# One base inverse of 128 partitions in place of two of 64, in a gated delta rule with retention

## The chip, the cores and the metric

The kernel runs on one core of a Trainium2 chip. The metric is the device time of one execution in microseconds (us); lower is better. The engines are TensorE (PE in the profile, with PEld for its weight loads), VectorE (DVE), ScalarE (ACT), GpSimd (POOL, which also issues DMAs) and SyncE (SP, which issues most loads).

## What is computed

One layer over 512 tokens of width 1024: an input projection, two mixers (a gated delta rule with 8 heads, and a retention with 4), their gated sum, and a squared-ReLU MLP. The change lies in the delta rule. Of the reference, cut to it:

```python
lower = jnp.where(strict, jnp.einsum('bhncd,bhnmd->bhncm', k_beta, k) * decay, 0.0)
t_inv = lax.linalg.triangular_solve(lower, eye, left_side=True, lower=True, unit_diagonal=True)
u = jnp.einsum('bhncm,bhnme->bhnce', t_inv, v * beta[..., None])
...
def step(state, inp):
    qe, ww, uu, aqk, kd, ld = inp
    v_new = uu - jnp.einsum('bhck,bhkv->bhcv', ww, state)
    o = jnp.einsum('bhck,bhkv->bhcv', qe, state) + jnp.einsum('bhcm,bhmv->bhcv', aqk, v_new)
    state = state * ld[..., None, None] + jnp.einsum('bhck,bhcv->bhkv', kd, v_new)
    return state, o
```

`t_inv` is the inverse of a unit lower triangular matrix for each head and each chunk of tokens. The kernel works with chunks of 128 tokens: 8 heads x 4 chunks = 32 triangular matrices of 128 x 128.

## The kernel before

All products of activations with weights are made of three matmuls (`mm3`, lines 84 to 86), from a high and a low half of each operand. `weights` loads a tile of weights on the SP queue; line 117 (ACT) and line 118 (DVE) split it into `whi` and `wlo`, which have three buffers each. `feature_major` (lines 252 to 270) takes 512 columns of weights into four PSUM banks of the pool `psm`, or 256 columns into two; the pool has four banks. A group of 512 columns is 96 matmuls of 512 columns, one of 256 columns 48.

The delta rule is the block from line 681. Its steps, in the order in which the program is written (lines 932 to 954), are:

- `keys(g4)` for four heads at a time (g4 = 0, 1): projection (for g4 = 0 it was made earlier, in `first_keys`), convolution and SiLU (`conv_silu`: a memset on POOL at line 632, two ACT copies out of the bank at 635 and 640, three taps on DVE at 642, ACT at 643, DVE at 646), transposes to token rows, squares and `rsqrt` (from line 695), decays (ACT 665, PE 666, ACT 668), the products of keys (PE 710), and on DVE `mt` (713, kept in the tile `acc`) and `kd` (716).
- `base_inverse(g4, pool)` for the 16 matrices of four heads: the four diagonal blocks of 32 x 32 of each matrix are copied through DRAM scratch so that every block has a partition of its own (64 partitions: four DMAs at line 726, one at 732), 31 elimination steps of two DVE operations each follow (741 and 747), a copy that transposes (748), and the results go back through DRAM (749 and 750, then 753 into `rt`). All these DMAs are issued by POOL.
- `double_blocks(pool, scr, m0)` for 8 matrices (two heads): it loads `rn` (765) and puts blocks of 32 together to 64 and to 128 with small matmuls (780, 786, 789, 797, 801) and DVE copies between them.
- `values_queries(g2, pool)` for a pair of heads: 512 columns of values and 256 of queries, with `conv_silu`, transposes (323), and `at` (832).
- `recurrence(g2, ...)` over the four chunks of a pair: PE 862, 871, 880, 894 and 901, with DVE and ACT operations between them.
- `gated(g2, ...)`: 512 columns of the gate in `token_major` (four banks), ACT 604 into the tile `zz`, DVE 605 and 607; then transposes and the output product `ya_partial`.

Buffers that the steps share: the `mrb` of the first inverse has the slot `zz`, that of the second lies in `acc`; the inverse's `tmp` has the slot `vn`, of one buffer, which the recurrence uses for `vn`; `rn` and `qf` share two buffers; `c_raw` and `c_y` have two each.

The order of the instructions on each engine is fixed before the run, by a planner: it goes by the order of the program (raised at places with `high_priority`), takes first what is ready and has its buffers by its own account of time, and so lets later steps run ahead of earlier ones that wait. Each engine then works through its list in order.

Of the kernel before, what the change touches and what calls it, by code (L numbers as in the profile page):

```python
# [10 lines left out]
F32 = mybir.dt.float32  # L11
# [8 lines left out]
P = 128  # L20
# [40 lines left out]
def hybrid_block_kernel(ctx: ExitStack, tc: tile.TileContext, a: dict, out: bass.AP):  # L61
    nc = tc.nc
# [299 lines left out]
    rt = pa.tile([P, 32, P], F32, name="rt")  # L362
# [318 lines left out]
    with delta_rule:  # L681
        mt = acc.rearrange("p k t -> p (k t)").rearrange("p (n c) -> p n c", c=P)
        def keys(g4, pool):
            br2 = pool.tile([P, 16], F32, tag="br2", name="br2")
            ssk = pool.tile([P, 16], F32, tag="ssk", name="ssk")
            ns = slice(16 * g4, 16 * g4 + 16)
            pss = feature_major(w_in, xs, OFF_KA + g4 * 512, 512, 8) if g4 else first_keys
            for i in range(4):
                h = 4 * g4 + i
                conv_silu(pss[i], 8 + h, kf[:, h, :], pool)  # L690
                pt = to_tokens(kf[:, h, :])
                junk = pool.tile([P, 256], BF16, tag="junk", name="junk")
                sum_squares(pt, ssk[:, 4 * i : 4 * i + 4], junk)
                nc.scalar.copy(kd[:, 4 * h : 4 * h + 4, :], pt)
            nc.vector.tensor_scalar(ssk, ssk, EPS, None, ALU.add)
            r = rsqrt(ssk, 16, "k")
            nc.vector.tensor_copy(rk[:, ns], r)
            beta_g = beta[:, :, 4 * g4 : 4 * g4 + 4].transpose([0, 2, 1])
            nc.vector.tensor_tensor(
                br[:, ns].rearrange("p (h c) -> p h c", h=4), beta_g, r.rearrange("p (h c) -> p h c", h=4), ALU.mult  # L700
            )
            nc.vector.tensor_tensor(br2, br[:, ns], r, ALU.mult)
            nc.vector.tensor_tensor(rinv[:, ns], r, ssk, ALU.mult)
            for i in range(4):
                h = 4 * g4 + i
                dt = decays(h, pool)
                pk = psx.tile([P, 4, P], F32, tag="dl", name="dl", bufs=3)
                for c in range(4):
                    kc = kf[:, h, c * P : (c + 1) * P]
                    nc.tensor.matmul(pk[:, c, :], kc, kc, start=True, stop=True)  # L710
                for c in range(4):
                    n = 4 * h + c
                    nc.vector.scalar_tensor_tensor(
                        mt[:, n, :], pk[:, c, :], br2[:, 4 * i + c : 4 * i + c + 1], dt[:, c, :], ALU.mult, ALU.mult
                    )
                    nc.vector.tensor_scalar(
                        kd[:, n, :], kd[:, n, :], rk[:, n : n + 1], dt[:, c, P - 1 : P], ALU.mult, ALU.mult
                    )

        def base_inverse(g4, pool):  # L720

            scr_m, scr_r, scr_t = (dr.tile([4, 16, 1024], F32, tag=f"scr{i}", name="scr") for i in range(3))
            ns = slice(16 * g4, 16 * g4 + 16)
            for b in range(4):
                bs = slice(32 * b, 32 * b + 32)
                nc.gpsimd.dma_start(scr_m[b].rearrange("n (m c) -> m n c", m=32), mt[bs, ns, bs])
            if g4 == 0:
                mrb = pool.tile([64, 2, 1024], F32, tag="zz", name="mrb")
            else:
                mrb = acc[0:64, 0:4, :].rearrange("p (i k) t -> p i (k t)", i=2)  # L730
            mb, rb = mrb[:, 0, :], mrb[:, 1, :]
            nc.gpsimd.dma_start(mb, scr_m.rearrange("b n e -> (b n) e"))
            nc.gpsimd.memset(rb, 0.0)
            nc.gpsimd.memset(rb[:, 0:1024:33], 1.0)
            tmp = pool.tile([64, 256], F32, tag="vn", name="tmp")
            mb3 = mb.rearrange("p (m c) -> p m c", m=32)
            rb3 = rb.rearrange("p (c i) -> p c i", c=32)
            for j in range(31):
                nr, ni = 31 - j, j + 1
                t3 = tmp[:, : nr * ni].rearrange("p (c i) -> p c i", c=nr)  # L740
                nc.vector.tensor_tensor(
                    t3,
                    mb3[:, j, j + 1 : 32].unsqueeze(2).to_broadcast([64, nr, ni]),
                    rb3[:, j, 0:ni].unsqueeze(1).to_broadcast([64, nr, ni]),
                    ALU.mult,
                )
                nc.vector.tensor_tensor(rb3[:, j + 1 : 32, 0:ni], rb3[:, j + 1 : 32, 0:ni], t3, ALU.subtract)
            nc.vector.tensor_copy(mb3, rb3.transpose([0, 2, 1]))
            nc.gpsimd.dma_start(scr_r.rearrange("b n e -> (b n) e"), rb)
            nc.gpsimd.dma_start(scr_t.rearrange("b n e -> (b n) e"), mb)  # L750
            for b in range(4):
                bs = slice(32 * b, 32 * b + 32)
                nc.gpsimd.dma_start(rt[bs, ns, bs], scr_t[b].rearrange("n (m c) -> m n c", m=32))
            return scr_r

        pool_marks = []
# [1 line left out]
        def double_blocks(pool, scr_r, m0):  # L758

            rn = pool.tile([P, 8, 64], F32, tag="qf", name="rn", bufs=2)  # L760
            nc.gpsimd.memset(rn, 0.0)
            for b in range(3):
                bs = slice(32 * b, 32 * b + 32)
                cs = slice(32 * (b % 2), 32 * (b % 2) + 32)
                mark = nc.gpsimd.dma_start(
                    rn[bs, :, cs], scr_r[b, m0 % 16 : m0 % 16 + 8].rearrange("n (m c) -> m n c", m=32)
                )
            pool_marks.append(mark)

            def bank(w):  # L770
                ps = psx.tile([P, T], F32, tag="dl", name="dl", bufs=3)
                return ps[:, : 8 * w].rearrange("p (n c) -> p n c", n=8)

            pairs = [(slice(b, b + 32), slice(b + 32, b + 64)) for b in (0, 64)]
            ns = slice(m0, m0 + 8)
            y = pool.tile([P, 8, 64], F32, tag="dt", name="y")
            p1 = bank(32)
            for lo, hi in pairs:
                for n in range(8):
                    nc.tensor.matmul(p1[hi, n, :], mt[lo, m0 + n, hi], rn[lo, n, 0:32], start=True, stop=True)  # L780
            for lo, hi in pairs:
                nc.vector.tensor_copy(y[hi, :, 0:32], p1[hi])
            p2 = bank(32)
            for lo, hi in pairs:
                for n in range(8):
                    nc.tensor.matmul(p2[lo, n, :], y[hi, n, 0:32], rt[hi, m0 + n, hi], start=True, stop=True)
            hi = slice(32, 64)
            for n in range(8):
                nc.tensor.matmul(p2[hi, n, :], rt[hi, m0 + n, hi], y[hi, n, 0:32], start=True, stop=True)
            for lo, hi in pairs:  # L790
                nc.vector.tensor_scalar(rt[lo, ns, hi], p2[lo], -1.0, None, ALU.mult)
            hi = slice(32, 64)
            nc.vector.tensor_scalar(rn[hi, :, 0:32], p2[hi], -1.0, None, ALU.mult)
            lo, hi = slice(0, 64), slice(64, 128)
            p3 = bank(64)
            for n in range(8):
                nc.tensor.matmul(p3[hi, n, :], mt[lo, m0 + n, hi], rn[lo, n, :], start=True, stop=True)
            nc.vector.tensor_copy(y[hi], p3[hi])
            p4 = bank(64)
            for n in range(8):  # L800
                nc.tensor.matmul(p4[lo, n, :], y[hi, n, :], rt[hi, m0 + n, hi], start=True, stop=True)
            nc.vector.tensor_scalar(rt[lo, ns, hi], p4[lo], -1.0, None, ALU.mult)
# [127 lines left out]
            gate_rows(pss, rows, lambda t: zz[:, t, :])  # L930

        keys(0, pa2)
        scr = base_inverse(0, pa2)
        vq = values_queries(0, pa2)
        keys(1, pa2)
        double_blocks(pa2, scr, 0)
        og = None
        for g2 in range(4):
            rows = recurrence(g2, vq, pa2)
            if g2 == 0:  # L940
                double_blocks(pa2, scr, 8)
                scr = base_inverse(1, pa2)
            if g2 < 3:
                vq = values_queries(g2 + 1, pa2)
            if g2 == 1:
                double_blocks(pa2, scr, 16)
                double_blocks(pa2, scr, 24)
            if g2 in (1, 2):
                add_blocks(pool_marks[-1], 8 + 2 * g2)
            gated(g2, rows, pa2)  # L950
            if g2:
                ya_partial(g2 - 1, og)
            og = gated_features(rows, lambda f: na[:, f % 2 : f % 2 + 1])
# [467 lines left out]
```

## Time and profile before

| | us |
|---|---|
| time, three runs | 1362.62, 1362.79, 1366.61 (median 1362.79) |
| profiled execution, first to last instruction | 1362.5 |
| PE busy | 1347.0 |
| DVE busy | 912.8 |
| ACT busy | 651.7 |
| POOL busy | 109.4 |
| matmul instructions | 6685 |

The profiled execution's own time is its span, 1362.5 us; its execution is not told apart from the three in the first row, and what lies outside the span is about 0.3 us against the median. Busy time is the union of an engine's instructions. A row of a timeline has the start, the duration, the engine, the line, and "output<-inputs"; a row of groups has the count, the busy time and the mean of one in ns, and the idle time ahead of it with what ended it. In a row of waits stand the total, the number and the longest.

### The profile page before, as it was taken

How to read it: one execution, taken by the hardware profiler on the slowest of the kernel's cores; microseconds unless marked ns; L12 is line 12 of the kernel's file. 1: busy time of each engine (PE TensorE's matmuls, PEld its weight loads, DVE VectorE, ACT ScalarE, POOL GpSimd, SP SyncE). 2: the span in 40 equal slices, each digit the busy share in tenths (PEclk: the TensorE clock that was granted, in tenths of full speed). 3: DMA queues.
4: the chain of work that ended last, by engine and by line, in shares of the span. 5: the costliest groups of instructions: out<-in, count | busy, mean ns of one | idle time of the engine just before them, and what ended most of it. 6: DMA issues, size and time to landing. Idle time of an engine off the chain costs nothing.

```text
span 1362.5 us, 17876 instructions
## 1 busy us (share of the span) xinstructions
PE 1347.0 (99%) x6685; PEld 1110.7 (82%) x6685; DVE 912.8 (67%) x1606; ACT 651.7 (48%) x1204; POOL 109.4 (8%) x161
## 2 busy tenths in 40 slices
PE   9999999999999999999999999999999999999997
PEld 7888787788877888888888888888889888888886
DVE  5799899864665557567477577575775744828535
ACT  5977564624543322453453343343355736436441
POOL 2010310121011002000000100011101100000000
PEclk9999999999999999999999999999999999999999
DMA  5254715379458447775584782488639843625421
GB/s 178 64 154 133 202 43 180 117 153 238 108 124 169 110 147 158 190 240 193 131 255 132 192 263 93 154 217 182 199 117 238 224 154 110 197 95 169 132 86 62
DMA packets 101718, 214.70 MB, mean 158 GB/s; under 512 B 7158, under 2 KB 20624, under 8 KB 101120
## 3 DMA queue, kind: packets, MB, share of 16 engines
q1 hardware_dynamic: 85616, 170.41, 39.1%
q0 software_dynamic: 15280, 42.03, 17.0%
q8 instruction: 52, 0.85, 0.3%
q10 hardware_dynamic: 736, 1.12, 0.2%
q14 instruction: 34, 0.28, 0.1%
HBM read 207.77 MB, written 64.49 MB: 200 GB/s over the span
## 4 chain that ended last, share of the span: by engine, by line
PE 89%; DVE 5%; DMA 2%; ACT 2%; issue 1%; DVEq 0%; ACTq 0%
PE mm L84 18%; PE mm L85 18%; PE mm L86 18%; PE mm L242 10%; PE dl L242 10%; PE tr L323 3%; PE mm L456 2%; DVE wlo L118 1%; PE dl L86 1%; PE dl L85 1%; PE dl L84 1%; PE dl L901 1%; PE dl L871 1%; DVE c_y L642 1%; PE dl L880 1%; PE dl L862 1%
## 5 line engine op out<-in xcount | busy, mean ns | idle before, releaser
L118 DVE TENSOR_TENSOR wlo<-raw,whi 128x1024 fp32r<-128x1024 f32 x245 | 298.8, 1221 | 269.0 <-ACT whi L117 267.7
L117 ACT CAST whi<-raw 128x1024 fp32r<-128x1024 f32 x245 | 257.4, 1052 | 428.9 <-PE mm L85 243.4
L84 PE MATMUL mm<-actT,whi 128*128 128x512 f32 x480 | 190.1, 396 | 0.0
L85 PE MATMUL mm<-actT,whi 128*128 128x512 f32 x480 | 189.9, 396 | 0.0
L86 PE MATMUL mm<-actT,wlo 128*128 128x512 f32 x480 | 189.0, 395 | 0.0
L84 PEld LDWEIGHTS mm<-actT,whi 128*128 128x128 f32 x480 | 90.2, 188 | 18.7 <-ACT c_y L640 0.8
L86 PE MATMUL mm<-hn,wlo 128*128 128x512 f32 (+1 forms) x288 | 105.4, 366 | 0.0
L85 PE MATMUL mm<-hn,whi 128*128 128x512 f32 (+1 forms) x288 | 105.3, 366 | 0.0
L84 PE MATMUL mm<-hn,whi 128*128 128x512 f32 (+1 forms) x288 | 105.3, 366 | 0.0
L86 PEld LDWEIGHTS mm<-actT,wlo 128*128 128x128 f32 x480 | 90.3, 188 | 17.9
L85 PEld LDWEIGHTS mm<-actT,whi 128*128 128x128 f32 x480 | 90.3, 188 | 17.8
L84 PE MATMUL mm<-og,whi 128*128 128x512 f32 x256 | 99.7, 390 | 1.0 <-DVE zz L605 1.0
L85 PE MATMUL mm<-og,whi 128*128 128x512 f32 x256 | 99.6, 389 | 0.0
L86 PE MATMUL mm<-og,wlo 128*128 128x512 f32 x256 | 99.6, 389 | 0.0
L242 PE MATMUL mm<-whi,xsum 128*128 128x512 f32 x256 | 80.8, 389 | 0.0
L642 DVE SCALAR_TENSOR_TENSOR c_y<-c_raw,convw,c_y 128x512 f32<-128x512 f32 x96 | 69.7, 743 | 2.4 <-ACT c_y L640 1.8
L85 PEld LDWEIGHTS mm<-hn,whi 128*128 128x128 f32 x288 | 54.3, 189 | 8.8
L84 PEld LDWEIGHTS mm<-hn,whi 128*128 128x128 f32 x288 | 54.3, 189 | 8.7
L86 PEld LDWEIGHTS mm<-hn,wlo 128*128 128x128 f32 x288 | 54.3, 189 | 8.7
L84 PE MATMUL mm<-whi,actT 128*128 128x512 f32 x152 | 61.1, 402 | 0.1
L242 PE MATMUL dl<-whi,actT 128*128 128x512 f32 x192 | 61.1, 389 | 0.0
L242 PE MATMUL dl<-whi,ffq 128*128 128x512 f32 x192 | 61.0, 389 | 0.0
(345 smaller groups left out, 2608.8 us busy)
## 6 DMA issues: line engine op xcount, KB each, us to landing
raw<-in_w_in_dram SPq DMA_DIRECT2D x101, 512.0 KB, 4.3
raw<-sums SPq DMA_DIRECT2D x56, 512.0 KB, 4.2
raw<-in_w_up_dram SPq DMA_DIRECT2D x36, 512.0 KB, 4.6
sums<-in_w_in_dram SPq DMA_DIRECT2D x32, 512.0 KB, 5.6
sums<-sums POOLq DMA_DIRECT2D x28, 512.0 KB, 7.1
raw<-in_w_down_dram SPq DMA_DIRECT2D x26, 512.0 KB, 3.8
sums<-in_w_down_dram SPq DMA_DIRECT2D x24, 512.0 KB, 7.4
raw<-in_w_br_a_dram SPq DMA_DIRECT2D x16, 512.0 KB, 4.0
```

What stands on the lines that cost most here:

```text
L84: nc.tensor.matmul(ps, lh, rh, start=first, stop=False)
L85: nc.tensor.matmul(ps, lh, rl, start=False, stop=False)
L86: nc.tensor.matmul(ps, ll, rh, start=False, stop=last)
L117: nc.scalar.copy(hi[:, :n], raw[:, :n])
L118: nc.vector.tensor_tensor(lo[:, :n], raw[:, :n], hi[:, :n], ALU.subtract)
L242: m = nc.tensor.matmul(pss[t], lhs[i // 2], rhs[i % 2], start=first and k + i == 0, stop=k + i == 5, skip_group_check=not first,)
L323: nc.tensor.transpose(ps, src, ident)
L456: nc.tensor.matmul(ps[:, ts], ws[w][:, kk, f * P : (f + 1) * P], xs[x][:, k, ts], start=first and kk + i == 0, stop=kk == len(ks) - 1 and ...
L642: nc.vector.scalar_tensor_tensor(y, raw[:, j : j + T], tap(j), y, ALU.mult, ALU.add)
L862: nc.tensor.matmul(ks[:, hh, :], kf[:, h0 + hh, cs], state[:, hh, :], start=True, stop=True)
L871: nc.tensor.matmul(px[:, hh, :], rt[:, nn[hh], :], vx[:, hh, :], start=True, stop=True)
L880: nc.tensor.matmul(pc[:, hh, :], kd[:, nn[hh], :], vn[:, hh, :], start=True, stop=True)
```

## The change

The two inverses of 64 partitions become one of 128 partitions, for all 32 matrices. It stands behind `keys(0)` and `keys(1)`, which are now next to one another; `values_queries(0)` comes after it. The call behind the first recurrence goes. The stores into the scratch and the loads into `rt` stay as small as they were, and are eight each in one call. `mrb` has the slot `zz`.

```diff
-        def base_inverse(g4, pool):
-
-            scr_m, scr_r, scr_t = (dr.tile([4, 16, 1024], F32, tag=f"scr{i}", name="scr") for i in range(3))
-            ns = slice(16 * g4, 16 * g4 + 16)
+        def base_inverse(pool):
+
+            scr_m, scr_r, scr_t = (dr.tile([4, 32, 1024], F32, tag=f"scr{i}", name="scr", bufs=1) for i in range(3))
             for b in range(4):
                 bs = slice(32 * b, 32 * b + 32)
-                nc.gpsimd.dma_start(scr_m[b].rearrange("n (m c) -> m n c", m=32), mt[bs, ns, bs])
-            if g4 == 0:
-                mrb = pool.tile([64, 2, 1024], F32, tag="zz", name="mrb")
-            else:
-                mrb = acc[0:64, 0:4, :].rearrange("p (i k) t -> p i (k t)", i=2)
+                for g4 in range(2):
+                    ns = slice(16 * g4, 16 * g4 + 16)
+                    nc.gpsimd.dma_start(scr_m[b, ns].rearrange("n (m c) -> m n c", m=32), mt[bs, ns, bs])
+            mrb = pool.tile([P, 2, 1024], F32, tag="zz", name="mrb")
...
-            tmp = pool.tile([64, 256], F32, tag="vn", name="tmp")
+            tmp = pool.tile([P, 256], F32, tag="vn", name="tmp")
...
-                    mb3[:, j, j + 1 : 32].unsqueeze(2).to_broadcast([64, nr, ni]),
-                    rb3[:, j, 0:ni].unsqueeze(1).to_broadcast([64, nr, ni]),
+                    mb3[:, j, j + 1 : 32].unsqueeze(2).to_broadcast([P, nr, ni]),
+                    rb3[:, j, 0:ni].unsqueeze(1).to_broadcast([P, nr, ni]),
...
-            for b in range(4):
-                bs = slice(32 * b, 32 * b + 32)
-                nc.gpsimd.dma_start(rt[bs, ns, bs], scr_t[b].rearrange("n (m c) -> m n c", m=32))
+            for g4 in range(2):
+                ns = slice(16 * g4, 16 * g4 + 16)
+                for b in range(4):
+                    bs = slice(32 * b, 32 * b + 32)
+                    nc.gpsimd.dma_start(rt[bs, ns, bs], scr_t[b, ns].rearrange("n (m c) -> m n c", m=32))
...
-                    rn[bs, :, cs], scr_r[b, m0 % 16 : m0 % 16 + 8].rearrange("n (m c) -> m n c", m=32)
+                    rn[bs, :, cs], scr_r[b, m0 : m0 + 8].rearrange("n (m c) -> m n c", m=32)
...
         keys(0, pa2)
-        scr = base_inverse(0, pa2)
+        keys(1, pa2)
+        scr = base_inverse(pa2)
         vq = values_queries(0, pa2)
-        keys(1, pa2)
         double_blocks(pa2, scr, 0)
         og = None
         for g2 in range(4):
             rows = recurrence(g2, vq, pa2)
             if g2 == 0:
                 double_blocks(pa2, scr, 8)
-                scr = base_inverse(1, pa2)
```

## The prediction

> **What bounds the kernel now.** The page comes first, for the engine that is never free.
>
> ```profile
> span 1362.5 us, 17876 instructions
> ...
> PE 1347.0 (99%) x6685; PEld 1110.7 (82%) x6685; DVE 912.8 (67%) x1606; ACT 651.7 (48%) x1204; POOL 109.4 (8%) x161
> ```
>
> TensorE (PE) is busy for 99% of the span, VectorE (DVE) for 67%. The change leaves the matmuls as they are, so it can win only what PE now idles, and can lose by making PE idle. The windows by stage show where the idling is (columns: window, its length, then busy us of PE, PEld, DVE, ACT, POOL, granted clock, DMA share, GB/s). The stage of the delta rule, to which every changed line belongs, is 60 to 440 us; the first base inverse lies in 89 to 139, the second in 186 to 237.
>
> ```profile
> 89.00:139.00 50.00, 49.38 (x245) 39.95 (x245) 49.06 (x137) 37.51 (x112) 5.02 (x11) 1.00 0.44 139
> ...
> 186.00:237.00 51.00, 50.38 (x303) 40.53 (x303) 48.19 (x137) 26.78 (x63) 4.36 (x6) 1.00 0.46 146
> ...
> 60.00:440.00 380.00, 375.84 (x2120) 303.24 (x2119) 292.65 (x668) 207.16 (x498) 55.10 (x90) 1.00 0.57 146
> ```
>
> PE idles 380.00 - 375.84 = 4.2 us in the whole stage, 0.6 us around the second inverse. DVE is full in both windows (49.06 of 50, 48.19 of 51), yet PE hardly notices: it runs matmuls of later steps ahead of time. The list of PE's waits agrees; these are its longest in this stage, and the only one that touches the second inverse:
>
> ```profile
> PE dl L880 <- ACT vn L875: 1.2, 1, 1.2
> ...
> PE tr L323 <- DVE vt L607: 0.6, 1, 0.6
> ```
>
> So the question is not how much DVE work goes, but whether PE still has enough work to run ahead on while it waits for the one inverse that is left.
>
> **The change part by part.** *Removed: the second inverse.* Its 31 pairs and its copy, and, for the price of 128 instead of 64 partitions, one copy of each kind out of PSUM:
>
> ```profile
> L741 DVE TENSOR_TENSOR tmp<-acc 64x31 f32<-64x31 f32 (+15 forms) x31 | 10.2, 330 | 0.3
> L747 DVE TENSOR_TENSOR acc<-acc,tmp 64x31 f32<-64x31 f32 (+15 forms) x31 | 10.2, 329 | 0.2
> ...
> L748 DVE COPY acc<-acc 64x1024 f32<-64x1024 f32 x1 | 1.1, 1066 | 0.0
> ...
> L798 DVE COPY y<-dl 64x512 f32<-64x512 f32 x4 | 2.8, 695 | 4.0 <-PE dl L797 4.0
> L890 DVE COPY st<-dl 128x512 f32<-128x512 f32 x4 | 2.7, 686 | 3.2 <-PE dl L880 3.2
> ```
>
> 695 ns on 64 partitions, 686 on 128: the one inverse on 128 costs what one on 64 did, and 10.2 + 10.2 + 1.1 = 21.5 us of DVE goes. What it is worth to the end is what PE waited there: at most the 0.6 us above. I take -0.6. On the GpSimd queue (POOL) one load and two stores go (4 + 1 + 2 + 4 DMAs twice become 8 + 1 + 2 + 8) and two memsets; POOL is 8% busy: nothing.
>
> *Moved: keys(1) ahead of the inverse.* Now the inverse starts as soon as keys(0) is done; its chain, as POOL, DVE and the chain of work show it:
>
> ```profile
> 76.24 2.61 POOL L726 DMA_DIRECT2D scr<-acc  x4 [24.05 <-DVE kd L716]
> ...
> 83.91 0.56 POOL L732 DMA_DIRECT2D mrb<-scr  x1 [0.69 <-DMA scr<-acc]
> ...
> 138.00 1.03 POOL L749 DMA_DIRECT2D scr<-mrb  x1 [7.88 <-DVE br L702]
> ...
> 141.99 1.21 POOL L765 DMA_DIRECT2D rn<-scr  x2 [2.24 <-DMA scr<-mrb]
> ```
>
> ```profile
> 88.78 0.17 DVE L741 TENSOR_TENSOR tmp<-mrb 64x31 f32<-64x31 f32 x1
> ...
> 137.79 1.13 DVE L748 COPY mrb<-mrb 64x1024 f32<-64x1024 f32 x1
> ```
>
> ```profile
> 148.22 0.23 PE mm L86
> 148.45 0.24 PE mm L84
> 148.69 0.62 PE dl L780 x16
> ```
>
> From the last kd to the first step: 88.78 - 76.24 = 12.5 us. The steps: 138.9 - 88.8 = 50.1 us, of which 21.5 are its own (the first inverse has the same instructions); DVE puts other work between every two. From its end to the first matmul of double_blocks(0) on PE (line 780): 148.7 - 138.9 = 9.8 us.
>
> When will keys(1) be done? It takes the place that the values of head pair 0 have now: four convolutions whose last DVE step is the first row below. Then come the squares (the second and third row, keys(1) now: 132.7 - 130.0 = 2.7 us) and the chain of rsqrt, mt and kd (keys(0) now: from the fourth row to 76.2, 15.6 us).
>
> ```profile
> 92.76 0.68 DVE L646 SCALAR_TENSOR_TENSOR c_y<-c_raw,c_y 128x512 f32<-128x512 f32 x1
> ...
> 129.29 0.67 DVE L646 SCALAR_TENSOR_TENSOR kf<-c_raw,c_y 128x512 f32<-128x512 f32 x1
> ...
> 132.69 0.18 DVE L695 TENSOR_SCALAR ssk<-ssk 128x16 f32<-128x16 f32 x1 [0.28 <-ACT junk L657]
> ...
> 60.58 0.17 DVE L695 TENSOR_SCALAR ssk<-ssk 128x16 f32<-128x16 f32 x1
> ```
>
> 93.4, less some 2 us of inverse steps and vt products between these convolutions today, is 91.5; + 2.7 + 15.6 = 110. The inverse begins at 110 + 12.5 = 122.5, or a little later, since each bulk transfer now has 512 KB. Nearest rows (KB, median us to landing):
>
> ```profile
> mrb<-scr POOLq DMA_DIRECT2D x1, 256.0 KB, 4.3
> acc<-scr POOLq DMA_DIRECT2D x1, 256.0 KB, 5.8
> ...
> sums<-sums POOLq DMA_DIRECT2D x28, 512.0 KB, 7.1
> ```
>
> Between +0 and +2.8 us each way (7.1 - 4.3; the last adds while it lands); I take +1, nearer to the rows of the same tile. The Trainium skill (DMA: Bandwidth & Descriptors, section Anatomy of one DMA) gives 2.0 us plus bytes / 436e3 for such a transfer, an estimate of 2.6 us for 256 KB, where the row has 4.3, and 0.6 us more for 512 KB: by it the sum would be 0.8 us lower in all. The eight small stores are issued 0.65 us apart (2.61 / 4); the four of heads 0 to 3 can go early. Start: 123.5.
>
> How long the steps take has two ends: alone 21.5 us, or 50.1 as now. In between lie the values and queries of pair 0, whose convolutions wait until then, and the wlo splits that feed PE; DVE was full in the same way, so I take the row, 50. End 173.5; + 9.8 + 1 gives double_blocks(0) at about 184 instead of 148.7.
>
> *What covers PE until then.* Matmuls between the start of the first of these groups and double_blocks(0), and those of the gate of pair 0, by line 84 (85 and 86 issue as many):
>
> ```profile
> L84 PE MATMUL mm<-actT,whi 128*128 128x512 f32 x119 | 47.3, 398 | 0.0
> ```
>
> ```profile
> L84 PE MATMUL mm<-whi,actT 128*128 128x512 f32 x32 | 13.5, 421 | 0.0
> ```
>
> Before the recurrence there are 144 + 96 + 144 = 384 matmuls (pair 0, keys(1), pair 1). 119 x 3 less two not begun, 355, are done at 148.65; 29 and the gate's 96 are left, 125 x 0.23 (each one's time in the chain above) = 28.8 us, and four groups of transposes of pair 1's values, 4 x 0.44 = 1.8 us by such a group in the chain:
>
> ```profile
> 156.77 0.44 PE tr L323 x4
> ```
>
> 148.7 + 28.8 + 1.8: PE is covered until 179. It then waits 184 - 179 = 5 us; behind line 780 in its queue stand the rest of double_blocks(0) and the recurrence of pair 0, and everything of later pairs waits for these. After that the gate's banks empty into zz, which the inverse has just released (mrb has its slot), and the values of pair 2 fill the gaps of double_blocks and the recurrence: 0.
>
> *The banks.* keys(1) and the values of pair 0, with four PSUM banks each, now follow one another; today the queries, with two, stand between.
>
> ```profile
> L84 PE MATMUL mm<-actT,whi 128*128 128x512 f32 x45 | 17.8, 397 | 0.0
> ```
>
> ```profile
> 83.58 0.69 ACT L640 ACTIVATE c_y<-mm,convw 128x512 f32<-128x512 f32 x1
> ```
>
> 133 matmuls (45 + 44 + 44) have run by 82.4. Afterwards PE could run 96 of keys(1) and, in the two free banks and with three weight buffers, 36: the same point. The third bank comes free at 83.58 + 0.69 = 84.3. That is 1.9 us, less two groups of transposes of 0.44: +1.
>
> Sum: 1362.5 - 0.6 + 5 + 1 = 1367.9, and the runs' median (1362.79) lies 0.3 above the profiled span: **1368**.
>
> **Rivals.** *The cover holds.* The inverse stands ahead of the other DVE work in the program's order, and with keys(1) done there is less to put between. If its steps take under 45 us, the blocks come by 179 and only the banks' 1 us is left: 1362 to 1366. For it speaks the end of the first inverse, where sixteen steps took the 6.5 us from 131.2 to 137.75 (their groups in that window stand below); against it, that DVE had no gap in 89 to 139.
>
> ```profile
> L741 DVE TENSOR_TENSOR tmp<-mrb 64x192 f32<-64x192 f32 (+7 forms) x8 | 2.2, 274 | 0.0
> L747 DVE TENSOR_TENSOR mrb<-mrb,tmp 64x192 f32<-64x192 f32 (+7 forms) x8 | 2.2, 273 | 0.0
> ```
>
> *The banks do not empty.* The gate needs four banks, and those of pair 1 leave only as its convolutions run, on a DVE that the inverse holds until 173. POOL can do the same: its line 749 waits for the inverse's end, and a c_raw memset (line 632) that is planned behind it holds up the convolution that needs it. Today's sign of a bank that waits for DVE:
>
> ```profile
> 155.46 0.58 ACT L635 COPY c_raw<-mm 128x512 f32<-128x512 f32 x1 [2.47 <-DVE c_y L646]
> ```
>
> If two banks are blocked, only 36 of the gate's 96 matmuls can run ahead, and 60 x 0.23 = 13.8 us of cover falls away: 1368 + 13.8 = 1381.8, 1376 to 1382 with part of it. It decides as soon as fewer than about 80 of the 96 run before double_blocks(0).
>
> *Faster.* Today the recurrence of pair 1 starts and then stands still, since its vn shares the buffer of the inverse's tmp:
>
> ```profile
> 209.24 1.03 PE L871 MATMUL dl<-vt,rt 128*128 128x256 f32 x4
> ```
>
> ```profile
> 236.39 0.84 ACT L875 ACTIVATE vn<-dl,br 128x256 f32<-128x256 f32 x2
> ```
>
> Without the second inverse these 27 us go, pair 1 to 3 come earlier, and the waits at the stage's end can close. The bound is all of the stage's idle time, 4.2 us: 1358.3 if no new wait comes. It decides if the blocks of pair 0 come by 179 and the later waits of over 1 us vanish.
>
> *A slower clock.* PE's granted clock is 1.00 in every window above; before it is warm, the first matmuls of the same 512 columns take longer:
>
> ```profile
> L381 PE MATMUL warm<-warm 128*128 128x512 bf16 x18 | 8.0, 630 | 1.3 <-DVE warm L370 1.3
> ```
>
> A wait that cools PE would cost 630 - 398 = 232 ns on each matmul until it is warm (398 from the row of line 84 above); if that lasts for eight, 1.9 us: 1370. The longest wait here, 1.3 us, shows nothing of it. The Trainium skill (TensorE: Matmul & The Clock Gate, section Why this matters for your kernels) says that an idle gap over some 3 us drops the clock to half; no run here shows it yet, and my 5 us in one piece would be the first.
>
> That the change does not do what it says, because 128 partitions cost twice as much, the two copies above exclude.
>
> **How the numbers follow.** 0.3% (4.1 us) is about what a measurement of this kernel can tell from no change. Chances: the forecast, a wait of 3 to 9 us, 0.37; with the slower clock 0.05; the cover holds 0.29; the banks 0.20; faster 0.09. Slower by over 0.3% (above 1366.9): 0.05 + 0.20 + 0.33 of the forecast = 0.58. Faster (below 1358.7): 0.07 of the last. Within: 0.35. The range must take in the cover's 1362 and reach into both ends: 1360 to 1380 leaves out about 0.08 at the bottom and 0.10 at the top.
>
> **What would show it.** The page: DVE 21 us less busy, PE's busy time the same, the span longer. Steps 741 and 747 once, on 128 partitions, at 330 ns each, starting near 123 and ending near 173. Line 780 first near 184, with a PE wait of about 5 us ahead of it. An idle second at 82 to 85. The recurrence of pair 1 without a gap between lines 871 and 875. It is wrong if line 780 comes before 175, if PE's waits in 60 to 190 sum to under 2 us, or if the gate's matmuls stand still for full banks.

## The result, and the profile after

The changed kernel takes 1377.07 us (median of 4 runs, 1375.37 to 1380.57), the kernel before 1362.70 us beside it (4 runs, 1361.72 to 1366.61): a ratio of 1.0102, 95% interval 1.0083 to 1.0122. The change makes the kernel 1% slower. The forecast had the sign and the place of the loss; its size, 5.3 us, is too small against 14.4. The profiled execution is the slowest of the four, 1380.57 us with a span of 1378.9; the others' spans are 1373.6 to 1375.4, 3.5 to 5.3 us less. What follows accounts for the 16.4 us between the two profiled spans (1378.9 - 1362.5), 2 us more than lie between the medians. How long the wait at line 780 is in the three shorter executions, no trace shows.

The first two parts of the page of the changed kernel:

```profile
span 1378.9 us, 17806 instructions
...
PE 1351.6 (98%) x6685; PEld 1114.2 (81%) x6685; DVE 894.8 (65%) x1543; ACT 651.0 (47%) x1204; POOL 103.1 (7%) x156
...
PEclk9999989999999999999999999999999999999999
```

VectorE has 18.0 us less to do (912.8 - 894.8; 21 were forecast), and the span is longer. The row of the clock has an 8 in the slice from 172 to 207 us. The windows, with the columns of the prediction, put the loss in the stage of the delta rule, in two places:

```profile
89.00:139.00 50.00, 46.90 (x233) 37.95 (x232) 44.59 (x111) 35.73 (x99) 5.43 (x13) 1.00 0.55 162
60.00:440.00 380.00, 365.88 (x2048) 295.41 (x2047) 264.81 (x586) 197.55 (x475) 46.03 (x82) 0.98 0.53 138
```

```profile
181.00:184.00 3.00, 0.20 (x1) 0.00 (x0) 1.22 (x1) 1.04 (x1) 0.00 (x0) 0.86 1.02 397
184.00:187.00 3.00, 0.00 (x0) 0.00 (x0) 1.10 (x2) 1.73 (x4) 2.71 (x5) 0.50 1.04 338
187.00:190.00 3.00, 0.00 (x0) 0.00 (x0) 1.38 (x3) 0.33 (x1) 2.34 (x4) 0.50 1.08 361
190.00:194.00 4.00, 3.89 (x23) 3.28 (x24) 0.00 (x0) 0.00 (x0) 1.86 (x3) 0.50 0.56 109
194.00:198.00 4.00, 4.00 (x13) 3.12 (x13) 0.00 (x0) 0.00 (x0) 0.00 (x0) 0.65 0.00 0
198.00:202.00 4.00, 4.00 (x19) 3.34 (x18) 1.22 (x1) 1.05 (x1) 0.00 (x0) 1.00 0.00 0
```

TensorE now idles 14.1 us of the stage (380.00 - 365.88) instead of 4.2. Of that, 8.8 lie in 181 to 190, where it does next to nothing and the DMA share is above 1. After that it is busy, but at a clock of 0.50 and 0.65: in 194 to 198 it starts 13 matmuls, in 198 to 202, at 1.00, 19. TensorE's longest waits in the stage say for what:

```profile
PE dl L780 <- DMA rn<-scr: 8.9, 1, 8.9
PE mm L86 <- DVE wlo L118: 1.8, 1, 1.8
PE tr L323 <- DVE mrb L745: 0.9, 1, 0.9
...
PE dl L871 <- ACT junk L908: 0.7, 1, 0.7
```

The first is the forecast's wait at line 780, 8.9 us for 5. The path of the inverse on GpSimd's queue, on VectorE and on TensorE (the steps are lines 739 and 745 now, the copy 746, the stores 747 and 748, the loads of rn 765):

```profile
112.66 2.57 POOL L727 DMA_DIRECT2D scr<-acc  x4 [2.05 <-DVE kd L716]
118.99 0.10 POOL L632 MEMSET c_raw<- 128x3 f32 x1 [3.76 <-DVE c_y L646]
...
120.36 0.57 POOL L730 DMA_DIRECT2D mrb<-scr  x1 [0.67 <-issue]
...
177.22 1.01 POOL L747 DMA_DIRECT2D scr<-mrb  x1 [9.88 <-DVE mrb L745]
...
184.29 1.21 POOL L765 DMA_DIRECT2D rn<-scr  x2 [5.36 <-DMA scr<-mrb]
```

```profile
126.45 0.19 DVE L739 TENSOR_TENSOR tmp<-mrb 128x31 f32<-128x31 f32 x1 [1.73 <-DMA mrb<-scr]
...
176.95 1.15 DVE L746 COPY mrb<-mrb 128x1024 f32<-128x1024 f32 x1
```

```profile
180.81 0.39 PE L86 MATMUL mm<-whi,actT 128*128 128x512 f32 x1
190.11 1.03 PE L780 MATMUL dl<-rn,acc 32*32 32x32 f32 x16 [8.91 <-DMA rn<-scr]
...
192.51 0.63 PE L84 MATMUL mm<-actT,whi 128*128 128x512 f32 x1
192.94 0.63 PE L85 MATMUL mm<-actT,whi 128*128 128x512 f32 x1
...
197.28 0.39 PE L84 MATMUL mm<-actT,whi 128*128 128x512 f32 x1
```

The last stores of mt go out at 112.7, the steps begin at 126.45 and their copy ends at 178.10, and line 780 begins at 190.11. Cover ended at 181.2. Then matmuls start 0.43 us apart until 197, and 0.23 apart from there.

The account of the 16.4 us goes by the two pages. TensorE is idle for 27.3 us of the span (1378.9 - 1351.6) instead of 15.5 (1362.5 - 1347.0), 11.8 more, and the same 6685 matmuls keep it busy for 4.6 us more (1351.6 - 1347.0). Of the idle time 8.9 us are the wait at line 780; the other 2.9 are the small waits of this kernel less those of the kernel before. Of the 4.6, some 3 are the slow clock from 190.11 to 197.05 (13 matmuls of 0.43 in place of 0.23 are 2.6, the first ones are a little worse). Some 1.5 us more come from a second slow stretch, in which seven matmuls start 0.43 us apart or more. No wait of over 0.7 us stands between the two:

```profile
240.00:245.00 5.00, 5.00 (x60) 3.85 (x57) 3.10 (x10) 2.15 (x10) 0.00 (x0) 0.66 0.00 0
```

### The profile page after: what moved, and what is told of

It reads as the page before. It is cut to its first block, busy times and chain, and to the rows that moved or that the text cites. A ratio compares the mean times of both kernels' runs of the same rounds, so it can differ in the third digit from the quotient of the medians.

```text
span 1378.9 us, 17806 instructions
## 1 busy us (share of the span) xinstructions
PE 1351.6 (98%) x6685; PEld 1114.2 (81%) x6685; DVE 894.8 (65%) x1543; ACT 651.0 (47%) x1204; POOL 103.1 (7%) x156
## 4 chain that ended last, share of the span: by engine, by line
PE 84%; DVE 7%; DMA 4%; ACT 3%; issue 2%; DVEq 0%; ACTq 0%; POOL 0%; POOLq 0%; SPq 0%
PE mm L84 17%; PE mm L85 17%; PE mm L86 17%; PE mm L242 10%; PE dl L242 9%; PE tr L323 2%; PE mm L456 2%; DVE wlo L118 2%; DVE c_y L642 1%; PE dl L871 1%; PE dl L84 1%; PE dl L86 1%; PE dl L85 1%; PE dl L901 1%; PE dl L880 1%
## 5 line engine op out<-in xcount | busy, mean ns | idle before, releaser
L84 PE MATMUL mm<-actT,whi 128*128 128x512 f32 x480 | 192.9, 402 | 0.1
L85 PE MATMUL mm<-actT,whi 128*128 128x512 f32 x480 | 191.5, 399 | 0.0
```

Of the source, the lines that this page charges most:

```text
L84: nc.tensor.matmul(ps, lh, rh, start=first, stop=False)
L85: nc.tensor.matmul(ps, lh, rl, start=False, stop=False)
```

## The experiments

The theory after the result: the steps on VectorE, in their new place, end too late for the cover; the round trip of the blocks through DRAM is stretched by full DMA engines; the wait lowers the clock. The rivals: the new order of the keys itself costs the time, or the transfers of 512 KB do, or the work is only badly divided between VectorE and GpSimd.

**The steps left out.** The changed kernel with no step at all: its 32x32 blocks stay identities, so this kernel leaves the base of the inverse out. Order, tiles and transfers stay.

```diff
-            for j in range(31):
+            for j in range(0):
```

> The changed kernel without the 31 elimination steps (the computation is cut: the inverse of the 32 x 32 blocks is left as the identity); the order, the one inverse's transfers and its copy stay. Theory (TensorE runs out of work because the one inverse ends too late, and its clock falls in the wait): without the 51.7 us of steps double_blocks(0) comes near 140 us, no wait at line 780, clock 1.00 from 60 to 260 us, time 1359 to 1364. Rival (what costs is the order of the keys, two groups of four banks one after the other): the time stays at 1370 or more. Rival (the one round trip of 512 KB through DRAM): a wait of several us stays at line 780.

Measured: 1359.19 us (10 runs), ratio 0.9975 (0.9965 to 0.9984) to a before of 1363.00. The stage's window:

```profile
60.00:440.00 380.00, 377.47 (x2132) 306.45 (x2131) 263.26 (x539) 208.71 (x500) 48.20 (x84) 1.00 0.56 144
```

TensorE idles 2.5 us, with no wait at line 780. So with VectorE relieved of the steps neither the order nor the 512 KB transfers cost anything; the loss needs the steps. Leaving out all of them gains 3.8 us against the kernel before, and no more.

**The order alone.** The kernel before, with two inverses of 64 partitions, and keys(1) ahead of the first one.

```diff
         keys(0, pa2)
+        keys(1, pa2)
         scr = base_inverse(0, pa2)
         vq = values_queries(0, pa2)
-        keys(1, pa2)
```

> The kernel before with keys(1) moved ahead of the first inverse, and still two inverses of 64 partitions. Theory (the start of the only inverse sets the end): the first inverse still needs keys(0) alone, so it starts near 88 us, double_blocks(0) comes before 179 us, no wait at line 780, time 1360 to 1366. Rival (the order of the keys by itself, through the PSUM banks): 1368 or more, with waits of TensorE between 75 and 130 us.

Measured: 1382.87 us (4 runs), ratio 1.0141 (1.0124 to 1.0158). The theory missed, and the rival's time came; this is slower than the whole change. Of the rival's mechanism, full PSUM banks, the list of waits has 2.8 us (line 84 for line 640). Waits of TensorE, and two windows:

```profile
PE tr L323 <- DVE c_y L646: 5.3, 3, 2.3
PE tr L323 <- DVE qf L646: 3.7, 2, 2.0
...
PE dl L780 <- DMA rn<-scr: 2.7, 1, 2.7
```

```profile
100.00:120.00 20.00, 15.61 (x78) 12.14 (x76) 19.65 (x61) 13.76 (x36) 2.76 (x6) 1.00 0.21 54
120.00:140.00 20.00, 11.41 (x40) 8.44 (x41) 19.12 (x43) 10.47 (x33) 0.86 (x5) 0.50 0.03 4
```

Here line 780 has a small part. The steps begin at 88, as before, but now keys(1)'s mt and kd, the steps and the convolutions of pair 0 all want VectorE in 100 to 140; it is full (38.8 us of 40), and TensorE waits for convolutions in several pieces, from 120 on at a clock of 0.50. But a full VectorE alone doesn't make the loss: in the kernel before it is as full in these 40 us (39.1), and TensorE is busy for 39.4 of them:

```profile
100.00:120.00 20.00, 19.42 (x97) 15.86 (x96) 19.42 (x52) 15.92 (x47) 2.96 (x3) 1.00 0.50 158
120.00:140.00 20.00, 20.00 (x98) 16.25 (x96) 19.65 (x65) 15.38 (x50) 1.86 (x5) 1.00 0.49 157
```

So "the inverse starts too late" was too narrow. As I read the rows, with both keys first TensorE has less work at hand that doesn't hang on what VectorE still has to do, and whatever the order puts last is waited for. With the inverse last it is line 780, and with the inverse first the convolutions. This is argued; no run takes it apart.

**The inverse later still.** The changed kernel with the values and queries of pair 0 ahead of keys(1).

```diff
         keys(0, pa2)
+        vq = values_queries(0, pa2)
         keys(1, pa2)
         scr = base_inverse(pa2)
-        vq = values_queries(0, pa2)
```

> The changed kernel with the values and queries of pair 0 put ahead of keys(1), as in the kernel before, so that the one inverse of 128 partitions starts still later. Theory: keys(1) is done near 151 us, the steps start near 165 with less other work between them (30 to 50 us), line 780 comes at 207 to 227 and waits 26 to 46 us, since its cover of 480 matmuls ends near 180: 1390 to 1412. Rival (the round trip of 512 KB is the cost, not the start): 1373 to 1381 as in the changed kernel.

Measured: 1383.42 us (4 runs), ratio 1.0150 (1.0135 to 1.0166).

```profile
PE dl L780 <- DMA rn<-scr: 20.6, 1, 20.6
```

```profile
180.00:200.00 20.00, 3.15 (x21) 2.73 (x22) 13.32 (x35) 2.06 (x4) 6.54 (x11) 0.50 0.36 122
```

The direction is the theory's, the size is smaller (a wait of 20.6 us for 26 to 46, and a time some 7 us below its range): keys(1) was done earlier than assumed (stores of mt at 145.6, not 151), and with less beside them the steps took 33 us (157.6 to 190.8) instead of 50.5.

**The steps on GpSimd.** The changed kernel with the 62 operations of the steps there.

```diff
-                nc.vector.tensor_tensor(
+                nc.gpsimd.tensor_tensor(
                     t3,
...
-                nc.vector.tensor_tensor(rb3[:, j + 1 : 32, 0:ni], rb3[:, j + 1 : 32, 0:ni], t3, ALU.subtract)
+                nc.gpsimd.tensor_tensor(rb3[:, j + 1 : 32, 0:ni], rb3[:, j + 1 : 32, 0:ni], t3, ALU.subtract)
```

> The changed kernel with the 62 operations of the elimination on GpSimd in place of VectorE. No row of the traces prices them on GpSimd; the bounds are the 20.4 us that VectorE takes and three times that. Theory: with no other work between them they end before about 165 us if they take under 38 us in all, and then line 780 doesn't wait: 1359 to 1365. If they take over 60 us the wait grows over that of the changed kernel: 1385 or more. Rival (VectorE's load and not the inverse's end is the limit): the time falls below 1362 whatever the steps take.

Measured: 1389.44 us (4 runs), ratio 1.0197 (1.0182 to 1.0212). The steps take 45 us (125.9 to 170.7), between the two cases of the expectation (under 38 and over 60). The time is that of the longer case, but by another wait than the one it named: TensorE waits for a convolution.

```profile
PE tr L323 <- DVE c_y L646: 24.4, 2, 24.3
```

My first reading was the forecast's hazard of GpSimd's queue: the memset of c_raw (line 632) stands behind the steps. The next run moves that memset away.

```diff
-        nc.gpsimd.memset(raw[:, 0:3], 0.0)
+        nc.vector.memset(raw[:, 0:3], 0.0)
```

> The changed kernel with the steps on GpSimd and the small memset of c_raw on VectorE, so that no convolution stands behind the steps in POOL's queue. Theory, the 24.3 us of the run with the steps on GpSimd were that queue: the wait for c_y is gone; the steps still take some 45 us (126 to 171), line 780 can begin at 182 to 184, and TensorE comes to it at about 155 to 165 in its planned order, so 18 to 27 us of wait move to line 780: 1378 to 1390. Rival, with VectorE free the steps aren't late any more, as the run without steps has it: wait under 5 us and 1359 to 1366.

Measured: 1385.10 us (4 runs), ratio 1.0156 (1.0139 to 1.0173). TensorE's longest wait, and VectorE's:

```profile
PE tr L323 <- DVE c_y L646: 21.5, 1, 21.5
```

```profile
DVE mrb L746 <- POOL mrb L745: 16.7, 1, 16.7
```

That reading fell: the wait is still there, and only 0.4 us at line 780, so that the time lies in the theory's range by luck. The second row has the cause. The transposing copy of line 746 was left on VectorE; it waits for the last step, and the convolutions behind it in VectorE's queue wait with it. The run before had the same row, with 21.0 us. So the next run moves the copy as well (and holds back some copies, as in the run below).

```diff
-            nc.vector.tensor_copy(mb3, rb3.transpose([0, 2, 1]))
+            nc.gpsimd.tensor_copy(mb3, rb3.transpose([0, 2, 1]))
```

> The changed kernel with steps and copy on GpSimd, the memset of c_raw on VectorE, and the copies of the block sums held back for loads 23 to 28. Theory, the wait of 21.5 us for c_y was VectorE's copy that waits 16.7 us for the steps with convolutions behind it: it goes. The steps end near 164, the copy 1 to 4 us later, the round trip is 7 us as in the run with the held copies, and line 780 can begin at 172 to 176. The planned order has 367 of the wide matmuls ahead of line 780 in place of 480, so TensorE comes to it at 150 to 156: a wait of 16 to 25 us moves to line 780, 1377 to 1388. Rival, with VectorE's queue free TensorE comes to 780 later, behind the other pair's convolutions, and the wait is under 8 us: 1362 to 1372.

Measured: 1389.29 us (4 runs), ratio 1.0180 (1.0154 to 1.0206).

```profile
PE dl L780 <- DMA rn<-scr: 19.1, 1, 19.1
PE tr L323 <- DVE c_y L646: 5.7, 1, 5.7
```

Most of the wait has moved to line 780, 19.1 us for the theory's 16 to 25; 5.7 us of the wait for c_y stay, and the time is 1.3 us above the theory's range. The planned order has only 367 of the wide matmuls ahead of line 780, where the changed kernel has 480, and the steps end later on GpSimd than that order has use for.

In the kernel before, an inverse has more room. There, too, the steps went to GpSimd and the memset to VectorE, first without the copy of line 748:

> The kernel before, with the steps of both inverses on GpSimd and the memset of c_raw on VectorE. Theory, in the old order the first inverse has room (it starts near 88, 780 is at 148.6): the steps take 45 us on GpSimd against 49 among VectorE's other work, end near 133 to 136, and VectorE is relieved of 43 us of steps; line 780 doesn't wait more than before, and the time is 1359 to 1363 (all of the stage's idle TensorE time is some 4 us). Rival, GpSimd's own work (the select on at at 110, the loads and stores of the inverses) stands behind the steps and is late: waits of 5 us and more at the second inverse or the recurrence, 1366 to 1380.

Measured: 1412.95 us (4 runs), ratio 1.0354 (1.0338 to 1.0369). Neither side had it: the two waits are VectorE's queue, as above, once at each inverse; the second is 22.1 us. The first:

```profile
PE tr L323 <- DVE kf L646: 22.6, 1, 22.6
```

Then with the copy on GpSimd as well:

> The kernel before, with both inverses' steps and the transposing copy behind them on GpSimd, and the memset of c_raw on VectorE. In the run with the steps alone on GpSimd the copy stood in VectorE's queue and waited 21.0 and 21.1 us for them, with convolutions behind it, and TensorE waited 22.6 and 22.1. Theory, these two waits are that queue alone: they go with the copy; the steps end at 134, the copy 1 to 4 us later, line 780 can begin at 143 to 147, where TensorE comes to it at about 146; 43 us of steps are off VectorE, and the time is 1358 to 1364. Rival, other work that waits for GpSimd takes their place (the select on at, the loads of the blocks, the stores of mt): waits over 5 us, 1368 to 1390.

Measured: 1394.20 us (4 runs), ratio 1.0211 (1.0185 to 1.0237). The two waits fall to 3.7 and 2.9 us, and the theory's time doesn't come, since another takes their place. The rival had that, though neither this wait nor a time as long:

```profile
PE dl L880 <- ACT vn L875: 16.7, 1, 16.7
```

```profile
ACT vn L875 <- POOL acc L747: 20.8, 1, 20.8
```

The second inverse's tmp has the buffer of vn, so the recurrence of pair 1 stands until its last step (line 747). The kernel before has the same dependence on VectorE, 209 to 236, and there TensorE has work for it. In none of these runs are the steps better placed on GpSimd, in either order.

**The DMA engines kept free.** The changed kernel, without the paced copies of block sums (512 KB each) that go with loads 23 to 28, among them those issued at 173.45, 175.65 and 179.69; they come later, one with each later load.

```diff
-        if paced and i >= 13 and len(trickle) > later_copies[0]:
+        if paced and i >= 13 and not 23 <= i <= 28 and len(trickle) > later_copies[0]:
```

> The changed kernel, with the paced copies of the block sums held back for loads 23 to 28, so that they don't fill the DMA engines while the inverse's blocks go out and come back (176 to 190). Theory, full DMA engines stretch the round trip: the way from the end of the steps to line 780 falls from 12.0 to 9 to 10.5 us, the wait at 780 from 8.9 to 6 to 7.5, the time to 1373.5 to 1376. Rival, the round trip is as long as its own transfers and their issues make it: wait 8 to 9, time 1376 to 1379. A second rival: the copies that are held back come later and collide with something else, and the time is above 1379.

Measured: 1371.95 us (4 runs), ratio 1.0058 (1.0043 to 1.0073) to a before of 1363.59: 5.1 us faster than the changed kernel. First the transfers of the changed kernel (KB each, median us to landing), then of this one, then its wait and windows:

```profile
scr<-mrb POOLq DMA_DIRECT2D x2, 512.0 KB, 6.8
```

```profile
scr<-mrb POOLq DMA_DIRECT2D x2, 512.0 KB, 4.2
```

```profile
PE dl L780 <- DMA rn<-scr: 3.6, 1, 3.6
```

```profile
184.00:187.00 3.00, 3.00 (x22) 2.40 (x19) 1.60 (x3) 0.55 (x2) 3.00 (x5) 0.60 1.01 335
187.00:190.00 3.00, 3.00 (x13) 2.44 (x12) 0.00 (x0) 0.00 (x0) 1.40 (x3) 0.83 1.05 191
190.00:194.00 4.00, 4.00 (x19) 3.34 (x18) 1.23 (x1) 1.05 (x1) 0.00 (x0) 1.00 0.03 5
```

The stores take 4.2 us instead of 6.8, the way from the end of the copy to line 780 is 6.7 us (177.10 to 183.80) instead of 12.0, the wait 3.6 instead of 8.9, and the clock is back by 190. So between these two executions 5.3 us of the wait go with the copies, more than the theory said. But the execution of the changed kernel with a profile is its slowest: the two profiled spans differ by 9.3 us (1378.9 - 1369.6), the medians by 5.1, slower clock included. In the usual execution the copies' share of the wait is therefore likely under 5.3. The control is the kernel before with the same line:

> The kernel before, with the copies of the block sums held back for loads 23 to 28: a control. Theory, what the held copies gave the changed kernel (5.1 us) is the shorter round trip ahead of its wait at 780; the kernel before has no such wait, and its time stays at 1361 to 1365. Rival, the copies cost something wherever they run: 1357 to 1360.

Measured: 1366.29 us (10 runs) to 1363.15, ratio 1.0014 (0.9998 to 1.0029). The time is 1.3 us above the theory's range, and the interval takes in no change. It gains nothing there, so the gain belongs to the changed kernel, and by the rows above to its wait.

A last run holds loads 17, 18 and 29 back as well. In it a copy comes behind an addition that needs it, so this kernel leaves a block sum incomplete.

```diff
-        if paced and i >= 13 and not 23 <= i <= 28 and len(trickle) > later_copies[0]:
+        if paced and i >= 13 and i not in (17, 18, *range(23, 30)) and len(trickle) > later_copies[0]:
```

> The changed kernel, with the copies of the block sums held back for loads 17, 18 and 23 to 29, so that they are out of the way of the load of mrb too (119.9 to 126, DMA engines full in the run with loads 23 to 28 held) and of the loads of rn and rt. Theory, the wait at 780 is the sum of the transfers around the steps as far as they are stretched: the load of mrb falls from 6.1 us to 4 to 5, the steps start at 123.5 to 125 in place of 125.5, the wait falls from 3.6 us to 1.5 to 3, and the time is 1369 to 1371.5. Rival, the steps end when VectorE's other work lets them, wherever they start: wait 3 to 4, 1371.5 to 1373.5. Second rival, nine copies held back are late for their sums: above 1374.

Measured: 1377.94 us (5 runs), ratio 1.0106 (1.0086 to 1.0125). The steps began at 124.5 and their copy ended 1.0 us earlier, but TensorE came to line 780 earlier by as much (3.5 us of wait, not 3.6). The loss is later; the window of this kernel, then that of the run with loads 23 to 28 held:

```profile
260.00:440.00 180.00, 173.13 (x974) 140.69 (x972) 112.19 (x216) 80.94 (x178) 24.82 (x35) 0.99 0.72 175
```

```profile
260.00:440.00 180.00, 178.03 (x1008) 144.34 (x1007) 115.82 (x223) 84.86 (x187) 25.64 (x36) 1.00 0.71 170
```

TensorE idles 4.9 us more there (178.03 - 173.13), of the 5.6 us by which the span is longer (1375.2 - 1369.6). The second rival's number came, and the SP queue's waits and a window show by what:

```profile
SPq L136 <- DMA sums<-sums: 28.4, 1, 28.4
```

```profile
340.00:380.00 40.00, 35.03 (x151) 28.03 (x150) 18.56 (x37) 15.70 (x34) 1.07 (x3) 0.96 0.79 199
```

A held copy (line 136) waits on that queue for an addition, from 327.4 to 355.8, and the loads of weights behind it wait with it. TensorE's 5.0 us of idle time in 340 to 380 follow; the run with loads 23 to 28 held has 0.1 us there.

**Another buffer for mrb.** In the changed kernel the gate's first activation starts at 185.3, after mrb's stores have freed the slot zz. Here mrb has a buffer of vt.

```diff
-            mrb = pool.tile([P, 2, 1024], F32, tag="zz", name="mrb")
+            mrb = pool.tile([P, 2, 1024], F32, tag="vt", name="mrb", bufs=2)
```

> The changed kernel with mrb in a buffer of vt, in place of zz, so that the gate's first activation needn't wait for mrb's stores. In the changed kernel the gate's four banks are full at 181, and the activation that empties them starts at 185.3. Theory, TensorE has nothing to do at the wait because these banks are held: the activation starts at 181 to 183, later projections run in the wait, and the time falls to 1368 to 1375. Rival, the planned order has line 780 after 402 of the wide matmuls in place of 480 and ties TensorE to it anyway: it comes to line 780 near 165, waits 15 to 24 us for it, and the time is 1378 to 1390.

Measured: 1386.95 us (4 runs), ratio 1.0170 (1.0154 to 1.0185): the rival's time, not by the rival's wait.

```profile
PE tr L323 <- DVE vt L811: 13.3, 1, 13.3
```

```profile
DVE vt L811 <- DMA scr<-mrb: 4.0, 1, 4.0
```

The values of pair 1 write vt (line 811). They stand behind the steps, and then wait 4.0 us for mrb's stores; TensorE waits for them. The dependence has only moved, to work that is needed earlier. Whether a buffer of its own would help is open.

## Why the prediction was right, and where it fell short

**Removed.** VectorE's 21.5 us were priced at no more than 0.6 us of the end. No run takes away the second inverse alone; leaving out all steps, the first inverse's too, brings 3.8 us, so little was to be had, as forecast. The recurrence of pair 1 runs without its gap, as forecast (line 871 at 252.02, line 875 at 253.08), and that brought nothing, as the bound of 4.2 us had it.

**128 partitions.** One of the two groups of the steps, in the stage's window:

```profile
L739 DVE TENSOR_TENSOR tmp<-mrb 128x31 f32<-128x31 f32 (+15 forms) x31 | 10.4, 337 | 1.8 <-DMA mrb<-scr 1.7
```

337 ns, against 330: the number of partitions hardly counts.

**The wait at line 780.** The mechanism came as forecast. This is the term whose size failed: 5 us forecast, 8.9 measured in the profiled execution. By its parts:

| term | forecast | measured |
|---|---|---|
| keys(1) done (stores of mt) | 110 | 112.7 |
| steps begin | 123.5 | 126.45 |
| steps and copy | 50 | 51.6 |
| end of the copy to line 780 | 10.8 | 12.0 |
| line 780 can begin | 184 | 190.1 |
| TensorE is covered until | 179 | 181.2 |

Line 780 can begin 6 us later than forecast, and the cover lasts 2 us longer. Of the 6 us, 2.7 are keys(1), 1.6 the steps and 1.2 the way back; why keys(1) and the steps took longer stays open. From the stores of mt to the first step the forecast is right to within 0.3 us. The load of mrb stood behind two memsets of c_raw in GpSimd's queue, the first of which waited 3.76 us for a convolution on VectorE (the row at 118.99). That isn't new: in the kernel before the same memset waits 3.68 us, at 82.53, and stores and load start 7.7 us apart in both, so the 12.5 us of the prediction hold it. The way back was taken over from the kernel before, plus 1. There the DMA share is 0.63 to 1.15 between 136 and 151, so other transfers are in that price too; the run with the copies held back shows that without six of them the way is 6.7 us.

**The cover.** It held to 181.2, and the steps took 51.6 us, so the rival in which they take under 45 fell. The "sixteen steps" that spoke for it are sixteen operations, eight of the 31 steps.

**The sum and the range.** The sum added 5.4 us to the profiled span; the two spans differ by 16.4. Of the missing 11.0 us, 3.9 are the wait at line 780, 4.6 the longer busy time, nearly all of it at a slower clock, for which the sum had nothing, and 2.5 the other waits (2.9 for the sum's 1 - 0.6). The median, 1377, lies in the range in part by luck. The forecast's own waits of 3 to 9 us end at 1372 (4 us above 1368), and what reaches to 1377 was put there for the rival of blocked banks (1376 to 1382), which didn't come. The 0.3 us between span and median was misread, without effect on the sum: where an execution has both numbers, some 1.7 us lie outside the span (1380.57 and 1378.9), so the profiled execution of the kernel before was itself some 1.4 us above the median.

**The clock.** It was set down as a rival of 0.05, at 1.9 us for eight matmuls. It came, as some 3 us behind the wait and some 4.5 in all. The error was to give it a chance apart from the forecast's: a wait of 5 us and the clock that follows it are one case, and the sum should have held both. The Trainium skill (TensorE: Matmul & The Clock Gate, section Why this matters for your kernels) has a gap over some 3 us halve the clock; here waits of 3.6, 8.9 and 20.6 us in one piece gave windows at 0.60, 0.50 and 0.50, so the trace agrees. But so long a wait isn't needed: in the run with the order alone the clock is at 0.50 in 120 to 140, with no wait of over 2.3 us but several close together, and in the changed kernel at 0.66 in 240 to 245 behind one of 0.7.

**The banks.** The +1 at 82 to 85 didn't come:

```profile
80.00:100.00 20.00, 20.00 (x105) 16.84 (x105) 13.28 (x29) 17.17 (x58) 0.76 (x4) 1.00 0.57 170
```

Nor did the rival of blocked banks: all 480 matmuls of the cover ran before line 780.

**Not seen.** The first place of the loss, 3.1 us of idle TensorE in 89 to 139 where it was 0.6: with both keys ahead of the values, TensorE waits 1.8 us for a weight split and 0.9 us behind a step on VectorE. That this is the same shortage as the one that makes line 780 late is my reading of the run with the order alone, and not shown: no order was found in which both the convolutions and the inverse come in time. Nor did any version with the one inverse and its steps beat the kernel before: the best, with the copies held back, is 8.4 us behind it.

## What to carry to other kernels

Work removed from an engine that nobody waits for is worth nothing; what counts is when the one result that is left comes, against the work that covers it, and every store, load and queue on its way belongs into that date at the price of the busiest moment, not of a quiet one. A forecast wait of several microseconds on TensorE needs its slower clock added to it. An operation moved to another engine takes its neighbours' queues with it: look for the reader that stays behind and for the buffer that is shared.

## What the runs showed of the hardware

- The clock after a wait: at 0.50, matmuls of 512 columns start 0.43 us apart in place of 0.23, for 7 us from the restart after a wait of 8.9 us. After 3.6 us it is at 1.00 again 6 us from the restart or sooner. It can fall without a long wait: 0.50 in 120 to 140 of the run with the order alone, where no single wait is over 2.3 us.
- With paced copies of 512 KB beside them, stores of 512 KB landed in 6.8 us, with six of the copies held back in 4.2.
- The 62 operations of the steps took 45 us on GpSimd, other short work of its queue included. In the run with the memset moved, GpSimd's mean for 247 elements is 680 ns (line 745); on VectorE no step of the kernel before took over 414. In that run the operation of line 739 on 207 elements took 1.52 us at 130, with VectorE at work, and 0.54 at 155, while VectorE waited.
